# A decoder layer in fp32 on one core: the up-projection's attention half by Strassen from its second output pair on, and the merged rows' Strassen sums formed there and spilled

## The chip, the cores and the metric

The kernel runs on one core of a Trainium2 chip. The metric is the device time of one execution in microseconds; for the kernel before the median of three runs is 2653.76 us (2652.42 to 2656.70). One execution was also taken by the hardware profiler, which gives the page and the trace that are read below. Engines are TensorE (PE in the profile), VectorE (DVE), ScalarE (ACT), GpSimd (POOL) and SyncE (SP), which issues most DMAs.

## What is computed

One layer of a decoder trunk with 512 tokens and a model width of 2048, all in float32:

```
h   = RMSNorm(x)
[u | v_sgu | q | k | v_att | g_a | g_b] = h @ W_in
y_a = u * (tril(W_s) v_norm + b)            # 1024 wide, chunks of 128
y_b = stick-breaking attention(q, k, v_att) # 1024 wide, 8 heads
merged = sigmoid(g_a) * (y_a @ W_up_a) + sigmoid(g_b) * (y_b @ W_up_b)
x  += merged @ W_o
x  += (silu(gate) * up) @ W_ffn_out,   [gate | up] = RMSNorm(x) @ W_ffn_in
x  += sigmoid(RMSNorm(x) @ W_pg) * (p @ W_ple)
```

The change lies in the product `y_b @ W_up_b` (1024 to 2048 channels) and in how `merged` is handed to `W_o`.

## The kernel before

**Numbers and products.** Every float32 operand is kept as two parts that TensorE multiplies at full rate, a high part (ACT copies it into the type fp32r) and a low part (DVE subtracts the high part from the original). A product of two such operands is three matmuls, high by high, high by low and low by high (`mm3`, L296 to L298). Activations stand transposed, channels by tokens. The work is cut into units of 256 input channels by 256 output channels by all 512 tokens. One output pair, 256 output channels, is a `Pair`; a stage has eight of them (j = 0 to 7), or 22 in the FFN.

**Two kinds of unit.** A plain unit ("P") is four blocks of `mm3`, 12 matmuls of 512 columns. A Strassen unit ("S", Winograd's form) cuts the weight unit and the activation into 2 x 2 blocks and makes seven block products instead of eight; with `doubled=7` each is one matmul of 512 columns, which holds high and low part of the right operand side by side, and one of 256, the weight's low part by the high part (L701). So it is 14 matmuls, seven of each size. The seven products collect in PSUM over all units of the pair, and at its end `mix_doubled` (L746 to L797) joins them into the output: four copies on ACT (L757), and on DVE thirteen additions (L760), one of 512 columns and twelve of 256. Weights come two units at a time (a "double"), into one of three slots of high and low parts (`whi_75` and `wlo_76`, `whi_77` and `wlo_78`, `whi_79` and `wlo_80`), four landings ahead of them.

**Weights** (class `Weights`, L320 to L390). A plain double is one load on SP (L339), the high split on ACT (L366) and the low split on DVE (L363), 1024 columns each. A Strassen double is two loads on SP (L341 and L349), an accumulating DMA on POOL (L370) that makes two of the sums, two sums on DVE (L382), and splits of 1280 and of 512 columns.

**Right operands ("forms")** lie in the arena `parts`. A plain form (`plain_form`) takes two blocks of 1024 columns, a Strassen form (`late_form`) a double place of 2 x PLACE = 3584. `plain_first` (L542 on) serves it: the plain blocks are split first, so that plain pairs can use the form; then a second copy of the raw block is loaded, its sums are made on DVE (`tt`, L534), and three of the four sums are split by ACT (L286) and DVE (L287); the fourth sum overwrites a plain block, so it is split only after the form's last plain use (`use_plain`). A pair knows by `until` from which j on its unit is plain or Strassen. `tick()`, called once or more per unit, builds the next waiting form, fetches second copies (`seconds`) and runs actions that `after(n, ...)` put off by n ticks. The tile scheduler then orders each engine's instructions, with manual dependencies that keep the weights and the units in their places.

**The up-projection** (L1376 to L1402). For j = 0 to 7 it makes a pair from the attention half (b) and then one from the gating half (a), four plain units each. For each, the gate's raw block comes from DRAM on SP (`gsp`, L525), is scaled on DVE (`scaled`, L1250) and passed through a sigmoid on ACT (L1383). DVE multiplies it by the two halves of the product straight from PSUM (L1388, twice 512 columns). After a's pair DVE adds both (L1392, 1024 columns), and the merged row is stored to DRAM (L1370, `spill["mix", j]`). After j = 1 to 5 there is a pair of the small product `p @ W_ple` ("ple pair", 12 matmuls, stored on SP).

**W_o's stage** follows. Its right operands `ms` are Strassen forms of the merged rows, loaded from that DRAM copy. `HALF` says how many of its pairs use each plain: the first four rows for one pair, the others for two; the second copies are loaded and summed in the meantime. Its pairs end at L806 (`rest`) and L811 (`onto`). The FFN stage has eight Strassen units per output pair, and one L1430 for each.

## Time and profile before

| | |
|---|---|
| median of three runs | 2653.76 us |
| the profiled execution | 2652.22 us |
| its span in the trace | 2650.5 us |
| TensorE busy | 2635.0 us (99%) |
| VectorE busy | 2255.1 us (85%) |
| ScalarE busy | 1409.0 us (53%) |
| GpSimd busy | 451.5 us (17%) |
| L1392 (end of a j), first and last start | 833.8 and 999.7 us |

The profile counts an instruction as busy from its start to its end; matmuls overlap, so a busy TensorE can still lose time between them. "Idle before" with an arrow names what released an engine that had waited. A row of the timeline gives start, duration, engine, line, operation, output and inputs, sizes and count. L numbers are lines of the kernel before; in the changed kernel the same code stands some lines lower (L363 is L366 there, L366 is L369, L382 L385, L287 L290, L534 L540, L701 L717, L760 L776, L806 L822, L1250 L1266, L1388 L1424, L1392 L1429).

### The profile page before, as it was taken

Reading aid. Unit: us, or ns where it says so; the run is one execution under the profiler, and the core shown is the slowest. Engines: PE = TensorE matmul, PEld = TensorE weight load, DVE = VectorE, ACT = ScalarE, POOL = GpSimd, SP = SyncE. Lnnn points to the kernel's source line nnn. Section 1 sums busy time; section 2 is a strip of 40 time slices with the busy share of each in tenths; the row PEclk is TensorE's granted clock in tenths of the full one; section 3 lists DMA queues with packets and bytes.
Section 4 is the critical chain, followed back from the end, with each engine's and each line's share of the span. In section 5 each row is a group of like instructions: output and inputs, shape, how many; then the busy total and the mean of one; then the engine's idle time right before and its main releaser. Section 6 shows DMA issues by size and latency. Waiting matters only on the chain.

```text
span 2650.5 us, 42355 instructions
## 1 busy us (share of the span) xinstructions
PE 2635.0 (99%) x15202; PEld 2301.7 (87%) x15202; DVE 2255.1 (85%) x3856; ACT 1409.0 (53%) x2245; POOL 451.5 (17%) x559
## 2 busy tenths in 40 slices
PE   9999999999999999999999999999999999999999
PEld 7888888889998888888888888888888888889888
DVE  8687878787887558999888888888889989989898
ACT  7756565655554335466444444444445445455543
POOL 0222223232220001101111111111110211211010
PEclk9999999999999999999999999999999999999999
DMA  6777777677775669988888788888887989988794
GB/s 209 183 195 171 194 172 192 171 192 191 175 195 186 223 224 271 254 246 212 223 213 217 197 203 203 195 212 201 202 203 225 255 227 275 225 242 254 239 269 137
DMA packets 288130, 561.46 MB, mean 212 GB/s; under 512 B 26288, under 2 KB 133552, under 8 KB 287920
## 3 DMA queue, kind: packets, MB, share of 16 engines
q1 hardware_dynamic: 225856, 440.77, 50.6%
q0 software_dynamic: 61776, 117.47, 27.8%
q8 instruction: 119, 1.95, 0.3%
q14 instruction: 91, 0.75, 0.1%
q10 hardware_dynamic: 288, 0.52, 0.1%
HBM read 507.28 MB, written 51.38 MB: 211 GB/s over the span
## 4 chain that ended last, share of the span: by engine, by line
PE 94%; DVE 3%; ACT 1%; DMA 1%; issue 1%; SPq 0%; DVEq 0%; ACTq 0%
PE ps L701 56%; PE ps L298 9%; PE ps L297 9%; PE ps L296 9%; PE small L701 6%; DVE wlo L363 1%; PE small L1181 1%; PE small L1129 1%; PE small L1055 1%; DVE parts L287 1%; DVE wholes L534 0%; DVE wholes L382 0%; PE small L1240 0%; DMA wholes<-x 0%; DMA wholes<-w_ffn_out 0%
## 5 line engine op out<-in xcount | busy, mean ns | idle before, releaser
L701 PE MATMUL ps<-parts,whi 128*128 128x512 f32 x4390 | 1470.6, 398 | 1.9 <-DVE out L806 0.8
L366 ACT ACTIVATE whi<-wholes 128x512 fp32r<-128x512 f32 (+2 forms) x934 | 873.1, 948 | 759.4 <-DVE wholes L382 308.6
L363 DVE TENSOR_TENSOR wlo<-wholes,whi 128x512 fp32r<-128x512 f32 (+2 forms) x934 | 980.8, 1086 | 78.5 <-ACT whi L366 77.6
L701 PEld LDWEIGHTS ps<-parts,wlo 128*128 128x128 f32 x4390 | 823.9, 188 | 188.0 <-DVE wlo L363 2.5
L701 PE MATMUL ps<-parts,wlo 128*128 128x256 f32 x4390 | 868.4, 279 | 1.1 <-DVE wlo L363 1.1
L701 PEld LDWEIGHTS ps<-parts,whi 128*128 128x128 f32 x4390 | 707.2, 189 | 11.3 <-issue 3.1
L297 PE MATMUL ps<-parts,whi 128*128 128x256 f32 (+1 forms) x1622 | 538.4, 332 | 1.0 <-DVE parts L287 0.9
L298 PE MATMUL ps<-parts,wlo 128*128 128x256 f32 (+1 forms) x1622 | 538.3, 333 | 1.1 <-DVE wlo L363 1.1
L296 PE MATMUL ps<-parts,whi 128*128 128x256 f32 (+1 forms) x1612 | 532.5, 332 | 1.8 <-ACT parts L286 1.4
L382 DVE TENSOR_TENSOR wholes<-wholes 128x256 f32<-128x256 f32 x820 | 346.3, 422 | 15.8 <-DVE wlo L363 0.4
L760 DVE TENSOR_TENSOR out<-out,ps 128x256 f32<-128x256 f32 x525 | 216.8, 416 | 152.2 <-ACT out L757 152.0
L297 PEld LDWEIGHTS ps<-parts,whi 128*128 128x128 f32 x1622 | 305.9, 189 | 37.9 <-DVE parts L287 2.9
L298 PEld LDWEIGHTS ps<-parts,wlo 128*128 128x128 f32 x1622 | 306.2, 189 | 30.6 <-DVE wlo L363 1.5
L296 PEld LDWEIGHTS ps<-parts,whi 128*128 128x128 f32 x1612 | 303.5, 189 | 32.2 <-ACT parts L286 2.2
L370 POOL DMA_DIRECT2D wholes<-w_ffn_in x169 | 147.6, 873 | 704.2 <-DVE wholes L382 209.7
L370 POOL DMA_DIRECT2D wholes<-w_in x132 | 117.0, 888 | 543.1 <-DMA wholes<-w_in 112.3
L701 PE MATMUL small<-parts,whi 128*128 128x512 f32 x480 | 190.2, 397 | 0.0
L757 ACT ACTIVATE out<-ps 128x256 f32<-128x256 f32 x279 | 104.7, 385 | 57.0 <-PE ps L701 52.9
L287 DVE TENSOR_TENSOR parts<-wholes,parts 128x1024 fp32r<-128x1024 f32 (+3 forms) x139 | 124.0, 904 | 12.6 <-ACT parts L286 12.5
L286 ACT ACTIVATE parts<-wholes 128x1024 fp32r<-128x1024 f32 (+3 forms) x139 | 107.8, 797 | 46.5 <-DVE wholes L534 32.4
L370 POOL DMA_DIRECT2D wholes<-w_ffn_out x64 | 55.9, 873 | 356.0 <-DMA wholes<-w_ffn_out 84.7
L1428 ACT ACTIVATE out<-out 128x512 f32<-128x512 f32 x44 | 27.9, 633 | 156.2 <-DVE out L1427 156.2
(135 smaller groups left out, 1833.6 us busy)
## 6 DMA issues: line engine op xcount, KB each, us to landing
wholes<-w_ffn_in SPq DMA_DIRECT2D x169, 384.0 KB, 5.6
wholes<-w_in SPq DMA_DIRECT2D x132, 384.0 KB, 5.0
wholes<-w_ffn_in SPq DMA_DIRECT2D x169, 256.0 KB, 4.8
wholes<-w_ffn_in POOLq DMA_DIRECT2D x169, 256.0 KB, 5.4
wholes<-w_in SPq DMA_DIRECT2D x132, 256.0 KB, 4.1
wholes<-w_in POOLq DMA_DIRECT2D x132, 256.0 KB, 5.0
wholes<-w_ffn_out SPq DMA_DIRECT2D x64, 384.0 KB, 6.0
wholes<-x SPq DMA_DIRECT2D x46, 512.0 KB, 6.1
```

The costliest lines, as they stand in the source:

```text
L286: return (nc.scalar.activation(hi, src, AF.Copy), nc.vector.tensor_tensor(out=lo, in0=src, in1=hi.bitcast(F32), op=ALU.subtract))
L287: nc.vector.tensor_tensor(out=lo, in0=src, in1=hi.bitcast(F32), op=ALU.subtract))
L296: nc.tensor.matmul(ps, sh, mh, start=start, stop=False)
L297: nc.tensor.matmul(ps, sh, ml, start=False, stop=False)
L298: return nc.tensor.matmul(ps, sl, mh, start=False, stop=stop)
L363: in_turn(nc.vector.tensor_tensor(out=self.lo[:, blocks], in0=r, in1=h.bitcast(F32), op=ALU.subtract))
L366: in_turn(nc.scalar.activation(h, r, AF.Copy))
L370: nc.gpsimd.dma_start(out=raw[:, 3:5], in_=self.src[:, 1:3], accum_op=ALU.add)
L382: in_turn(nc.vector.tensor_tensor(out=o, in0=x, in1=y, op=ALU.add))
L701: m = nc.tensor.matmul(out, l, r, start=first and k == 0, stop=last and k == 1)
L757: in_turn(nc.scalar.activation(out, x, AF.Copy, scale=scale))
L760: in_turn(nc.vector.tensor_tensor(out=out, in0=x, in1=y, op=op))
```

## The change

- **Attention half by Strassen.** `W_up_b` is planned as "SSSS" for j = 1 to 7, and the four forms of `y_b` become Strassen forms with `until` 1: b's pair is plain at j = 0 and Strassen for the seven pairs after. The pair's result comes out of `mix_doubled` in SBUF, and one multiply of 1024 columns (L1421) takes the place of the two of 512. The second copy of each `y_b` block comes from its DRAM copy.
- **Room.** The four double places for b and the plain blocks for a share the arena `parts`; the high part of a's first form is taken at the arena's other end, behind the last place (`how=("high", "low")`).
- **Sums of the merged rows.** After each j, `leave` makes the row's four Strassen sums on DVE (three instructions, L540: one of 512 columns, two of 256) in the block that held b's part, stores them to DRAM on SP (`sum_spill`, L1436) and then stores the row itself (L1402). W_o's Strassen forms load those sums (L1385 and L1386, 768 and 256 columns) in place of a raw second copy, and only split them. `tick` waits with that load until the sums have been stored, and asks for the smaller rooms.

```diff
--- before.py
+++ after.py
@@ -222,8 +222,11 @@
             builds.popleft().step()
         if seconds:
             f = (urgent or seconds)[0]
-            if (f.used or not any(b.stage == f.stage and b.ready() and not b.there
-                                  for b in builds)) and fits([(wholes, 5 * 256, "old")]):
+            need = [768, 256] if f.sums else [5 * 256]
+            if f.ready_second() and (
+                    f.used or not any(b.stage == f.stage and b.ready() and not b.there
+                                      for b in builds)) and fits(
+                        [(wholes, n, "old") for n in need]):
                 f.fetch_second()
         while waiting and waiting[0][0] <= clock[0]:
             heapq.heappop(waiting)[2]()
@@ -452,12 +455,14 @@
     class Form(Staged):
 
 
-        def __init__(self, kind, steps, sizes, ready, src=None, far=False):
+        def __init__(self, kind, steps, sizes, ready, src=None, far=False, sums=None,
+                     ready_second=lambda: True):
             super().__init__(steps(self))
             self.kind, self.sizes, self.ready = kind, sizes, ready
             self.blocks, self.at_plain, self.used = None, kind == "P", False
             self.src, self.there, self.block, self.due = src, not far, None, 0
             self.second, self.due_second, self.forced, self.stage = None, 0, False, -1
+            self.sums, self.ready_second = sums, ready_second
 
         def fetch(self):
             self.block, self.there, self.due = self.src(), True, clock[0] + WAIT
@@ -469,7 +474,8 @@
         def fetch_second(self):
             if self in seconds:
                 seconds.remove(self)
-            self.second, self.due_second = self.src(5 * 256), clock[0] + WAIT
+            self.second = self.sums() if self.sums else self.src(5 * 256)
+            self.due_second = clock[0] + WAIT
 
         def second_arrived(self):
             if self.forced and self.second is None:
@@ -556,6 +562,15 @@
         yield
         while not form.second_arrived():
             yield
+        if form.sums:
+            t, v = form.second
+            split_into(x[:, 4:7, 0], x[:, 4:7, 1], cut(t.f()))
+            give(t)
+            while not form.used:
+                yield
+            split_into(x[:, 3, 0], x[:, 3, 1], v.f())
+            give(v)
+            return
         w = form.second
         b = cut(w.f())
         if gain:
@@ -603,7 +618,7 @@
         split_into(x[:, 3, 0], x[:, 3, 1], v.f())
         give(v)
 
-    def late_form(src, ready=always, gain=None, far=False):
+    def late_form(src, ready=always, gain=None, far=False, **how):
 
 
 
@@ -615,11 +630,11 @@
             return form.operand()
 
         return Form("S", steps, [(parts, 2 * PLACE, "place"), (wholes, 1024, "low")], ready,
-                    src, far)
-
-    def plain_form(src, ready=always, gain=None, raw=1024, how="low", far=False):
+                    src, far, **how)
+
+    def plain_form(src, ready=always, gain=None, raw=1024, how=("low", "low"), far=False):
         def steps(form):
-            hi, lo = form.blocks = parts.take(1024, how), parts.take(1024, how)
+            hi, lo = form.blocks = tuple(parts.take(1024, h) for h in how)
             w = form.raw()
             if gain:
                 gained(hi.own(), w.f(), *gain)
@@ -636,7 +651,8 @@
             return tuple([x.own(0, T), x.own(T)] for x in form.blocks)
             yield
 
-        return Form("P", steps, [(parts, 1024, how)] * 2 + [(wholes, raw, "low")] * bool(raw),
+        return Form("P", steps,
+                    [(parts, 1024, h) for h in how] + [(wholes, raw, "low")] * bool(raw),
                     ready, src, far)
 
     class Pair:
@@ -1300,7 +1316,8 @@
     def plan_rest():
         for j in range(KU):
             for b in "ba":
-                plan((w_up_a if b == "a" else w_up_b)[j], "PPPP")
+                plan((w_up_a if b == "a" else w_up_b)[j],
+                     "SSSS" if b == "b" and j else "PPPP")
             if 0 < j < 6:
                 planned.append((w_ple[j + 2].rearrange("p (b c) -> p b c", b=4), 1, "P"))
         for j in range(KU):
@@ -1316,9 +1333,11 @@
             plan(w_gate[j], now(GATE, GATE_UNTIL, j))
 
     def y_form(c, i):
-        return plain_form((lambda: y_a[i]) if c == "a" else lambda: load(y_spill[i]),
-                          lambda: len(y_done) == 8, raw=0 if c == "a" else 1024,
-                          far=c == "b")
+        if c == "b":
+            return late_form(lambda n=1024: load(y_spill[i], n), lambda: len(y_done) == 8,
+                             far=True)
+        return plain_form(lambda: y_a[i], lambda: len(y_done) == 8, raw=0,
+                          how=("low" if i else "high", "low"))
 
     ys = {(c, i): y_form(c, i) for c in "ba" for i in range(4)}
     build(ys.values())
@@ -1359,7 +1378,20 @@
     part = {}
     spill = {(n, j): tc.dram_tile([P, 1024], F32, name=nm(n)) for n in ("mix", "x1", "x2")
              for j in range(KU)}
-    there = set()
+    there, sum_spill = set(), {}
+
+    def second_blocks(d):
+        blocks = take(768, "old"), take(256, "old")
+        nc.sync.dma_start(out=blocks[0].f(), in_=d[:, 256:1024])
+        nc.sync.dma_start(out=blocks[1].f(), in_=d[:, 0:256])
+        return blocks
+
+    def summed_form(kind, n, j):
+        if kind == "P":
+            return spilled_form(kind, n, j)
+        d = sum_spill[n, j] = tc.dram_tile([P, 1024], F32, name=nm(n))
+        return spilled_form(kind, n, j, sums=lambda: second_blocks(d),
+                            ready_second=lambda: (n, j, "sums") in there)
 
     def spilled_form(kind, n, j, gain=None, **how):
         return (late_form if kind == "S" else plain_form)(
@@ -1371,7 +1403,7 @@
         there.add((n, j))
         give(block)
 
-    ms = [spilled_form("S", "mix", j) for j in range(KU)]
+    ms = [summed_form("S", "mix", j) for j in range(KU)]
     build(ms)
     for j in range(KU):
         for b in "ba":
@@ -1383,15 +1415,30 @@
                 nc.scalar.activation(g, g, AF.Sigmoid)
 
             after(1, gate)
-            pr = pair([ys[b, i] for i in range(4)], last=j == KU - 1)
-            for h, ps in zip((g[:, :T], g[:, T:]), pr.ends()):
-                nc.vector.tensor_tensor(out=h, in0=h, in1=ps, op=ALU.mult)
+            pr = pair([ys[b, i] for i in range(4)], last=j == KU - 1, j=j,
+                      until=(b == "b",) * 4, doubled=7 * (b == "b"))
+            if pr.n["S"]:
+                nc.vector.tensor_tensor(out=g, in0=g, in1=pr.o, op=ALU.mult)
+            else:
+                for h, ps in zip((g[:, :T], g[:, T:]), pr.ends()):
+                    nc.vector.tensor_tensor(out=h, in0=h, in1=ps, op=ALU.mult)
             if b == "b":
                 part[j] = s
             else:
-                nc.vector.tensor_tensor(out=g, in0=g, in1=part[j].f(), op=ALU.add)
-                give(part.pop(j))
-                after(1, lambda j=j, s=s: store("mix", j, s))
+                other = part.pop(j)
+                nc.vector.tensor_tensor(out=g, in0=g, in1=other.f(), op=ALU.add)
+
+                def leave(j=j, s=s, other=other):
+                    o, x = cut(other.f()), cut(s.f())
+                    tt(o[:, 0:4:3], twice(x[:, 3]), x[:, 1:3])
+                    tt(o[:, 1], o[:, 3], x[:, 1])
+                    tt(o[:, 2], o[:, 1], x[:, 0], ALU.add)
+                    nc.sync.dma_start(out=sum_spill["mix", j], in_=other.f())
+                    give(other)
+                    store("mix", j, s)
+                    there.add(("mix", j, "sums"))
+
+                after(1, leave)
         if not j:
             ple_operands()
         elif j < 6:
```

## The prediction, on record before the changed kernel ran

> **What bounds the kernel now.** I read the page first: the span, the engines, the chain that ended last.
>
> ```profile
> span 2650.5 us, 42355 instructions
> PE 2635.0 (99%) x15202; PEld 2301.7 (87%) x15202; DVE 2255.1 (85%) x3856; ACT 1409.0 (53%) x2245; POOL 451.5 (17%) x559
> PE 94%; DVE 3%; ACT 1%; DMA 1%; issue 1%; SPq 0%; DVEq 0%; ACTq 0%
> ```
>
> The matmul stream is the time: a change pays by taking matmul time off PE, and loses only where PE is made to wait. The profiled run took 2652.22 us, 1.72 around its span and 1.54 below the median 2653.76; the sum below is a difference, put on the median at the end.
>
> Then the stage. First the starts of L1392, which closes each j; then stretches of two j of the up-projection and one FFN output pair (start:end, length, busy time and count of PE, PEld, DVE, ACT, POOL; clock, DMA share, GB/s); then L1430, once per FFN pair of eight Strassen units.
>
> ```profile
> 953.49 1.22 DVE L1392 TENSOR_TENSOR wholes<-wholes 128x1024 f32<-128x1024 f32 x1
> 977.97 1.23 DVE L1392 TENSOR_TENSOR wholes<-wholes 128x1024 f32<-128x1024 f32 x1
> 999.73 1.22 DVE L1392 TENSOR_TENSOR wholes<-wholes 128x1024 f32<-128x1024 f32 x1
> ```
>
> ```profile
> 857.30:881.80 24.50, 24.50 (x109) 20.29 (x109) 16.37 (x20) 9.57 (x12) 0.00 (x0) 1.00 0.65 225
> 1500.00:1519.50 19.50, 19.50 (x113) 17.04 (x112) 17.28 (x32) 9.37 (x13) 3.49 (x4) 1.00 0.76 194
> ```
>
> ```profile
> L1430 DVE TENSOR_TENSOR out<-out x3: 682/684/686, 1505.3 to 1544.4; 128x512 f32<-128x512 f32 x3
> ```
>
> A j takes 24.48 us with a ple pair (96 + 12 matmuls of 512 columns) and 21.76 without: both give 0.2267 us per matmul, at clock 1.00, PE never idle. What PE waits for, in the up-projection (809 to 999.5) and around w_o's start (1000 to 1060):
>
> ```profile
> PE ps L297 <- DVE parts L287: 0.5, 1, 0.5
> PE ps L701 <- DVE out L806: 0.8, 1, 0.8
> ```
>
> **What a Strassen pair saves.** A plain pair of four units is 48 x 0.2267 = 10.88 us. FFN pairs come every (1544.4 - 1505.3) / 2 = 19.55 us for eight units, 9.77 for four. So 1.11 us per pair, 7.8 us for the seven b pairs of j = 1 to 7.
>
> A rule speaks against this. The Trainium skill, page "TensorE: Matmul & The Clock Gate", section "Back-to-back issue gap", gives a sustained spacing of about 131 ns at 512 columns and 81 at 128, so that small matmuls pay a floor; by my estimate from these, about 98 ns at 256, seven products of one of each would cost 1.60 us against 1.57 for twelve of 512, and nothing would be saved. Here it does not hold: 0.2267 us per 512-column matmul, and 14 matmuls in 2.44 us, 0.349 per pair of sizes, hence about 0.12 for the 256-column one. That is nearer the same page's isolated gap, N/2.4 + 2.5, which gives 216 and 109 ns.
>
> **What it costs on DVE.** DVE runs an instruction while the one before drains, so I count steps from start to start:
>
> ```profile
> 812.94 0.42 DVE L760 TENSOR_TENSOR out<-out,ps 128x256 f32<-128x256 f32 x1
> 813.27 0.69 DVE L760 TENSOR_TENSOR out<-ps,out 128x512 f32<-128x512 f32 x1
> 813.87 1.22 DVE L363 TENSOR_TENSOR wlo<-wholes,whi 128x1024 fp32r<-128x1024 f32 x1
> 815.00 1.22 DVE L1250 TENSOR_TENSOR wholes<-wholes 128x1024 f32<-128x1024 f32 x1
> L363 DVE TENSOR_TENSOR wlo<-wholes,whi 128x1280 fp32r<-128x1280 f32 x410 | 609.7, 1487 | 21.4 <-ACT whi L366 20.9
> ```
>
> 0.335 for 256 columns, 0.60 for 512, 1.14 for 1024; so about 1.42 for 1280 and 0.87 for 768 (estimates, by the same 0.07 to 0.08 under a duration). The dear place is the build of b's Strassen operands: their sums and second splits can be made only between the last plain use (j = 0) and the first Strassen use (j = 1). DVE in order, from the last product of b at j = 0 to a's second multiply; before, then now (L540 sums, L290 low halves, L385 and L366 weights, L1424 is old L1388, L1429 old L1392):
>
> ```order
> L363 TENSOR_TENSOR wlo_78<-wholes,whi_77 128x1024
> L287 TENSOR_TENSOR parts<-wholes,parts 128x512 x2
> L1388 TENSOR_TENSOR wholes<-wholes,ps_8366 128x512
> L1388 TENSOR_TENSOR wholes<-wholes,ps_8367 128x512
> L1392 TENSOR_TENSOR wholes<-wholes 128x1024
> ```
>
> ```order
> L366 TENSOR_TENSOR wlo_78<-wholes,whi_77 128x512
> L540 TENSOR_TENSOR wholes<-wholes 128x2x256
> L540 TENSOR_TENSOR wholes<-wholes 128x256 x2
> L1424 TENSOR_TENSOR wholes<-wholes,ps_8381 128x512
> L540 TENSOR_TENSOR wholes<-wholes 128x2x256
> L290 TENSOR_TENSOR parts<-wholes,parts 128x4x256
> L366 TENSOR_TENSOR wlo_76<-wholes,whi_75 128x1024
> L1424 TENSOR_TENSOR wholes<-wholes,ps_8382 128x512
> L540 TENSOR_TENSOR wholes<-wholes 128x256
> L1429 TENSOR_TENSOR wholes<-wholes 128x1024
> L540 TENSOR_TENSOR wholes<-wholes 128x256
> L290 TENSOR_TENSOR parts<-wholes,parts 128x4x256
> ```
>
> The first two forms straddle the end of j = 0; the splits of the third and fourth stand 8 and 10 rows further down, with the spill sums and a gate between. What DVE does there before:
>
> ```profile
> 821.05 2.36 DVE L287 TENSOR_TENSOR parts<-wholes,parts 128x1024 fp32r<-128x1024 f32 x2 [0.26 <-ACT parts L286]
> 831.79 0.69 DVE L1388 TENSOR_TENSOR wholes<-wholes,ps 128x512 f32<-128x512 f32 x1 [0.80 <-PE ps L298]
> 833.08 0.69 DVE L1388 TENSOR_TENSOR wholes<-wholes,ps 128x512 f32<-128x512 f32 x1 [0.60 <-PE ps L298]
> 833.81 1.22 DVE L1392 TENSOR_TENSOR wholes<-wholes 128x1024 f32<-128x1024 f32 x1
> 856.95 1.22 DVE L1392 TENSOR_TENSOR wholes<-wholes 128x1024 f32<-128x1024 f32 x1
> ```
>
> From 813.87 to L1392 of j = 1 at 856.95 it has 43.1 us. Before, 18 steps of 1024, 11 of 512 and 4 of 256 stand there: 28.5 us. Now 4 of 1280, 19 of 1024, 1 of 768, 19 of 512, 30 of 256: 49.7 us. So this queue runs at least 6.6 us late at the end of j = 1. PE does not see all of it. The multiply at 833.08 had waited for the last matmul of j = 0, so b's second pair began near 832.9, and j = 1 ended near 832.9 + 21.76 = 854.6. With no idle on DVE, the first split (19.7 us of steps) is done at 833.6, just after that start; the fourth (31.6 us) at 845.5. With 1 to 3.5 us of waits on ACT and PE, of the kind of the bracketed 0.26, 0.80 and 0.60, the fourth is done at 846.5 to 849. PE fills some of the gap: its order puts the products on unsummed operands first, and eight matmuls of a's pair into b's second double. After the fourth split are still to run some 2.8 us of b's products (four of seven of a 4.88 us double) and 40 matmuls of a, 9.07 us: j = 1 ends at 858.4 to 860.9 if all of them wait for that split, at 853.5 if nothing waits. More of a is drawn forward around the earlier waits, since PE's order holds pieces of both pairs there, so I take 857.5, +2.9, which holds the first saved pair. Bounds: +6.3, and -1.6 with all hidden, the 0.5 at L297, whose splits change in the same stretch, gone too.
>
> In the steady j the mix comes in:
>
> ```order
> L1392 TENSOR_TENSOR wholes<-wholes 128x1024
> L363 TENSOR_TENSOR wlo_80<-wholes,whi_79 128x1024
> L363 TENSOR_TENSOR wlo_78<-wholes,whi_77 128x1024
> L1250 TENSOR_TENSOR wholes<-wholes 128x1024
> L1388 TENSOR_TENSOR wholes<-wholes,ps_8751 128x512
> ```
>
> ```order
> L1429 TENSOR_TENSOR wholes<-wholes 128x1024
> L540 TENSOR_TENSOR wholes<-wholes 128x2x256
> L776 TENSOR_TENSOR out_8924<-out_8924,ps_8882 128x256
> L540 TENSOR_TENSOR wholes<-wholes 128x256
> L776 TENSOR_TENSOR out_8924<-out_8924,ps_8887 128x256
> L540 TENSOR_TENSOR wholes<-wholes 128x256
> L776 TENSOR_TENSOR out_8924<-out_8924 128x256
> ```
>
> The spill sums stand between the first steps of the next mix (old L760), so their store leaves SP some 3 us into b's pair, and the Strassen weights and gates queued behind it on SP wait as long. A j has 7 steps of 1024 and 5 of 512 before, 11.0 us; now 2 of 1280, 6 of 1024, 7 of 512, 18 of 256, 19.9, against a period of 24.48 - 1.11 = 23.37. It fits, with 3.5 us over, so the late queue catches up within two j. The last two hold 22.7 of 23.37 and 19.6 of 20.65. What else DVE waited for in one j before:
>
> ```profile
> 863.92 1.23 DVE L363 TENSOR_TENSOR wlo<-wholes,whi 128x1024 fp32r<-128x1024 f32 x1 [2.60 <-ACT whi L366]
> 867.11 1.23 DVE L1250 TENSOR_TENSOR wholes<-wholes 128x1024 f32<-128x1024 f32 x1 [1.97 <-DMA wholes<-gsp]
> 869.46 1.28 DVE L1388 TENSOR_TENSOR wholes<-wholes,ps 128x512 f32<-128x512 f32 x2 [1.12 <-ACT wholes L1383]
> 875.79 1.23 DVE L363 TENSOR_TENSOR wlo<-wholes,whi 128x1024 fp32r<-128x1024 f32 x1 [2.07 <-ACT whi L366]
> ```
>
> 7.8 us of idle, mostly DVE being early; I price what stays of it at 0.1 us of PE wait per j, 0.7 in all, between 0 and 0.5 each (3.5).
>
> **w_o's start.** The sums of the merged rows leave DVE there, and the 0.8 us at L701 with them: -0.8, between 0 and -1.0. DMA: the up-projection's own traffic (809 to 1000), the page's GB/s by slices, and what a double of Strassen weights takes in the FFN, against a plain one:
>
> ```profile
> DMA packets 12055, 40.51 MB, mean 212 GB/s; under 512 B 1316, under 2 KB 1759, under 8 KB 12044
> ...
> GB/s 209 183 195 171 194 172 192 171 192 191 175 195 186 223 224 271 254 246 212 223 213 217 197 203 203 195 212 201 202 203 225 255 227 275 225 242 254 239 269 137
> ...
> wholes<-w_ffn_in SPq DMA_DIRECT2D x169, 384.0 KB, 5.6
> wholes<-w_ffn_in SPq DMA_DIRECT2D x169, 256.0 KB, 4.8
> wholes<-w_ffn_in POOLq DMA_DIRECT2D x169, 256.0 KB, 5.4
> ...
> wholes<-w_up_b SPq DMA_DIRECT2D x13, 512.0 KB, 5.1
> ```
>
> Fourteen doubles gain 384 KB each, and eight stores of 512 KB come in: 9.7 MB more make 263 GB/s, below the busiest slice's 275. Free, or part of the 0.7. ACT (9.57 of 24.50 us busy) takes the longer high halves and four copies per mix, POOL (0.00) the accumulates: free.
>
> **Sum:** 2.9 - 6 x 1.11 + 0.7 - 0.8 = -3.9; on the profiled run 2648.3, on the median 2649.9. The bounds together: -9.3 to +3.1.
>
> **Rivals.** *The build hides.* PE's reordering covers the queue: -1.6 - 6.7 - 0.8 = -9.1, 2644.7. For it: a's 10.88 us of plain work are there to be drawn forward; against: the 6.6 us overflow, and that the order draws only eight of 48. *DVE becomes the bound* of the stage: the idle of 7.8 us per j stays, since the gates come behind a store that waits for DVE itself. Each us of idle beyond 3.5 costs one per j. From 4.3 us on the change is a loss, from 5.2 on one that a measurement tells (6 x 1.7 + 2.9 - 6.7 - 0.8 = +5.6); at 6 us it is +10.4, 2664.2. For it: the order of store and gates on SP; against: with the queue behind, splits and gates have arrived before DVE gets to them. *The matmul floor*, with nothing saved per pair: +4.0 + 0.7 - 0.8 = +3.9, 2657.7; the rows above leave it 0.03.
>
> **Numbers.** Forecast 0.62, hidden build 0.20, DVE bound 0.15, floor 0.03. A measurement of this kernel tells 0.2%, 5.3 us: under 2648.5 is faster, over 2659.1 slower. Of the forecast's cases about a quarter lie under 2648.5. Faster 0.20 + 0.15 = 0.35; slower 0.12, most of the DVE bound; same 0.53. The range runs from near the hidden build to the early end of the DVE bound: 2645.0 to 2656.5.
>
> **What would show it.** Right: L1429 16 to 23.5 us apart but 24 to 30 at j = 1; PE waits of 3 to 6 us on L290 or L776 in b's second pair and none beyond 0.5 later; no L822 wait at w_o's start. Wrong: waits on L366, L1266 or gates in j = 3 to 7, no wait at j = 1, or pairs not 1.1 us shorter.

## The result, and the profile after

The changed kernel is slower: 2678.4 us against 2656.06 (medians of six runs each), a ratio of 1.0085 with a 95% interval of 1.0075 to 1.0096. The forecast was 2649.9, with a range of 2645.0 to 2656.5. The profiled execution took 2678.21 us, 26.0 more than that of before (2652.22), which lies below all six of its timed runs; so its profile shows a little more loss than the medians do.

From the page of the changed kernel, the span, the engines, and the chain that ended last by engine:

```profile
span 2676.3 us, 42772 instructions
PE 2638.9 (99%) x15258; PEld 2301.1 (86%) x15258; DVE 2317.8 (87%) x3992; ACT 1430.8 (53%) x2292; POOL 465.6 (17%) x573
PE 80%; DVE 9%; DMA 7%; issue 2%; ACT 2%; SPq 0%; DVEq 0%; ACTq 0%; POOLq 0%
```

PE still reads 99% busy. What moved is the chain, from 94% PE to 80%, with 9% DVE and 7% DMA. The add that closes each j (L1429) as a group, with first and last start:

```profile
L1429 DVE TENSOR_TENSOR wholes<-wholes x8: 1218/1222/1227, 839.4 to 1021.0; 128x1024 f32<-128x1024 f32 x8
```

And the one of j = 1, from the timeline:

```profile
871.34 1.23 DVE L1429 TENSOR_TENSOR wholes<-wholes 128x1024 f32<-128x1024 f32 x1
```

Against 833.8, 856.95 and 999.7 before, the add of j = 0 comes 5.6 us later, that of j = 1 14.4 and that of j = 7 21.3. These are DVE's times, and DVE is behind PE here. PE's own last matmul of a's pair (found by its place in the program's order) ends at 861.9 in j = 1 and at 1016.6 in j = 7, against 854.8 and 999.0 before: 7.1 and 17.6 us later. So from j = 1 to 7 PE lost another 10.5 us, where six Strassen pairs should have won 6.7, 17.2 in all. What PE waits for in the up-projection (800 to 1022; in all, times, longest):

```profile
PE ps L717 <- DVE wholes L1424: 5.0, 3, 4.0
PE ps L717 <- DVE wlo L366: 3.3, 3, 1.5
PE ps L299 <- DVE out L776: 2.9, 1, 2.9
PE ps L717 <- ACT out L918: 2.5, 5, 0.8
PE ps L299 <- ACT parts L289: 1.6, 1, 1.6
PE ps L300 <- DVE parts L290: 0.8, 2, 0.5
PE ps L717 <- DVE parts L290: 0.4, 1, 0.4
```

These add up to 16.5 us, where there were 0.5 before. The splits of b's own operands, on which the prediction had set its 2.9, are the 0.4 of the last row. The large ones are a's multiply (L1424), which frees PSUM banks, and the low halves of weights (L366). Both stand in DVE's queue, and what DVE itself waited for longest in this stretch is the gate; first the changed kernel's row, then the one of before (800 to 1000):

```profile
DVE wholes L1266 <- DMA wholes<-gsp: 18.8, 7, 4.0
```

```profile
DVE wholes L1250 <- DMA wholes<-gsp: 13.2, 9, 2.3
```

Why the gate is late shows in the chain that ended last, between j = 5's add and b's and a's multiplies of j = 6 (968 to 1002; start, duration, what):

```profile
972.40 1.14 DVE wholes L1429
...
974.68 0.60 DVE wholes L540
...
976.78 0.42 DVE wholes L540
...
977.24 8.30 DMA mix<-wholes
...
985.55 3.74 DMA wholes<-gsp
...
992.34 1.13 DVE wholes L1421
...
996.62 0.61 DVE wholes L1424
...
997.27 2.52 PE ps L717 x8
```

The add, the spill sums, their store (8.30 us to landing), then the load of the next gate into the block that was just stored, the scaling, the multiplies, and PE. `take(..., "low")` gives the lowest free block, and that is the one whose store is under way: two blocks serve nearly all of the sixteen gates in turn. Before, the block of b's part was free right after the add, with no store behind it. The stores have also become slower, with the sums and the Strassen weights beside them (in the up-projection; KB each, median us to landing; the changed kernel, then the one of before):

```profile
mix<-wholes SPq DMA_DIRECT2D x14, 512.0 KB, 6.3
```

```profile
mix<-wholes SPq DMA_DIRECT2D x7, 512.0 KB, 2.8
```

Three of PE's waits cost more than themselves. In the stretches behind them (start:end, length, busy PE, PEld, DVE, ACT, POOL; granted clock, DMA share, GB/s) the clock is down:

```profile
846.20:851.20 5.00, 4.99 (x17) 4.07 (x18) 3.27 (x4) 1.51 (x2) 0.83 (x1) 0.66 0.71 94
892.00:895.00 3.00, 3.00 (x11) 2.26 (x9) 2.96 (x5) 2.36 (x3) 0.00 (x0) 0.50 0.09 32
997.20:1001.20 4.00, 3.93 (x14) 3.40 (x15) 3.93 (x6) 1.32 (x2) 0.00 (x0) 0.57 0.69 217
```

That is 5.00 x 0.34 + 3.00 x 0.50 + 4.00 x 0.43 = 4.9 us of matmul time, none of which was in the sum. PE, again, shows as busy in them. With the 7.8 us that were saved, PE lost 25.4 us in the up-projection: the waits name 16.0 of them and the clock 4.9, and 4.5 are not named by any view.

Nor does the loss end there. W_o's first and seventh outputs (L811, L827 in the changed kernel) come 16.3 and 18.1 us later than before, and the whole span is 25.8 us longer. So some 8 us of the loss arise behind the up-projection. PE's waits from 1016.6 on add up to 8.8 us there, against 3.3 us from 999.0 on before.

### The profile page after: what moved, and what is told of

Read it like the earlier page. It is cut to its first block, busy times and chain, and to the rows that moved or that the text cites. A ratio compares the mean times of both kernels' runs of the same rounds, so it can differ in the third digit from the quotient of the medians.

```text
span 2676.3 us, 42772 instructions
## 1 busy us (share of the span) xinstructions
PE 2638.9 (99%) x15258; PEld 2301.1 (86%) x15258; DVE 2317.8 (87%) x3992; ACT 1430.8 (53%) x2292; POOL 465.6 (17%) x573
## 4 chain that ended last, share of the span: by engine, by line
PE 80%; DVE 9%; DMA 7%; issue 2%; ACT 2%; SPq 0%; DVEq 0%; ACTq 0%; POOLq 0%
PE ps L717 55%; PE small L717 6%; PE ps L301 5%; PE ps L300 5%; PE ps L299 5%; DVE wlo L366 3%; DVE parts L290 1%; DMA wholes<-gsp 1%; DVE wholes L540 1%; DMA wholes<-x 1%; DMA wholes<-w_o 1%; DMA mix<-wholes 1%; DMA wholes<-hid 1%; DVE out L776 1%; DVE wholes L385 1%
## 5 line engine op out<-in xcount | busy, mean ns | idle before, releaser
L717 PE MATMUL ps<-parts,whi 128*128 128x512 f32 x4558 | 1531.1, 399 | 10.1 <-DVE wholes L1424 5.0
L366 DVE TENSOR_TENSOR wlo<-wholes,whi 128x512 fp32r<-128x512 f32 (+2 forms) x948 | 994.2, 1085 | 40.2 <-ACT whi L369 39.5
L717 PE MATMUL ps<-parts,wlo 128*128 128x256 f32 x4558 | 903.5, 279 | 6.0 <-DVE wlo L366 6.0
L300 PE MATMUL ps<-parts,whi 128*128 128x256 f32 (+1 forms) x1510 | 495.7, 329 | 3.1 <-DVE parts L290 2.9
L301 PE MATMUL ps<-parts,wlo 128*128 128x256 f32 (+1 forms) x1510 | 494.9, 329 | 1.8 <-DVE wlo L366 1.8
L299 PE MATMUL ps<-parts,whi 128*128 128x256 f32 (+1 forms) x1500 | 489.8, 329 | 6.9 <-ACT parts L289 3.0
L385 DVE TENSOR_TENSOR wholes<-wholes 128x256 f32<-128x256 f32 x848 | 359.9, 424 | 23.3 <-DMA wholes<-w_up_b 3.7
L776 DVE TENSOR_TENSOR out<-out,ps 128x256 f32<-128x256 f32 x567 | 234.6, 417 | 157.9 <-ACT out L773 157.5
L717 PE MATMUL small<-parts,whi 128*128 128x512 f32 x508 | 202.1, 398 | 0.0
```

The costliest lines, as they stand in the source:

```text
L299: nc.tensor.matmul(ps, sh, mh, start=start, stop=False)
L300: nc.tensor.matmul(ps, sh, ml, start=False, stop=False)
L301: return nc.tensor.matmul(ps, sl, mh, start=False, stop=stop)
L366: in_turn(nc.vector.tensor_tensor(out=self.lo[:, blocks], in0=r, in1=h.bitcast(F32), op=ALU.subtract))
L385: in_turn(nc.vector.tensor_tensor(out=o, in0=x, in1=y, op=ALU.add))
L717: m = nc.tensor.matmul(out, l, r, start=first and k == 0, stop=last and k == 1)
```

## The experiments

Each kernel was timed beside the kernel before on the same chip (medians of 2654.1 to 2654.7 there), and a ratio is to that. The theory after the traces: **A, the loop** (store, landing, gate load, multiply) makes the waits. Its rival: **B, DVE is simply full** with 20 us of steps per j.

**Sums left out, sums alone.** The first keeps the Strassen half and gives `other` back after L1429:

```diff
-    ms = [summed_form("S", "mix", j) for j in range(KU)]
+    ms = [spilled_form("S", "mix", j) for j in range(KU)]
...
                 nc.vector.tensor_tensor(out=g, in0=g, in1=other.f(), op=ALU.add)
+                give(other)
...
-                    tt(o[:, 0:4:3], twice(x[:, 3]), x[:, 1:3])
-                    tt(o[:, 1], o[:, 3], x[:, 1])
-                    tt(o[:, 2], o[:, 1], x[:, 0], ALU.add)
-                    nc.sync.dma_start(out=sum_spill["mix", j], in_=other.f())
-                    give(other)
                     store("mix", j, s)
-                    there.add(("mix", j, "sums"))
```

> The attention half by Strassen as changed, but no sums of the merged rows in the up-projection: W_o's forms load a raw second copy, as before the change, and the block of b's part is given back right after L1429. Theory A (the loop): a j's next gate is loaded into the block from which the sums are stored, so store, landing, gate load, sigmoid and multiply stand one behind the other, and PE waits for the multiply to free its PSUM banks; the waits from j = 2 on (about 17 us with the slow clock behind them) then nearly go: 2660 to 2667 us, about 14 less than the change's 2678. Theory B (DVE full): DVE's own 20 us of steps per j make the waits; this kernel takes only 1.3 us per j off, so 2670 to 2677.

Measured: 2670.5, ratio 1.0057 (1.0042 to 1.0072). Eight us less, at the low end of B. DVE's and PE's longest waits:

```profile
DVE wholes L1266 <- DMA wholes<-gsp: 21.3, 8, 4.8
PE ps L717 <- DVE parts L290: 7.0, 2, 6.4
```

The gate is as late as ever, but all of DVE's waits for it, save one of 1.0 us at the start, are now for b's gate, which has no store before it: it goes into the block that L1429 has just read, so it is loaded behind the add, and it takes 5.3 to 9.8 us to land. a's gate still stands behind the row's store, but DVE waits for it nowhere. So the loop closes without a store too: add, load, landing, multiply. Its price on PE fell all the same. From j = 1 to 7 PE takes 143.8 us instead of 154.7, so 6.3 are lost there instead of 17.2. The build of b's operands took much of that back, with a single wait of 6.4 us for a split; j = 1 ends on PE at 868.1 instead of 861.9. A's number failed, and this run alone does not tell A from B.

The second keeps the sums and their stores and leaves b plain:

```diff
-                     "SSSS" if b == "b" and j else "PPPP")
+                     "PPPP")
...
-            return late_form(lambda n=1024: load(y_spill[i], n), lambda: len(y_done) == 8,
-                             far=True)
+            return plain_form(lambda: load(y_spill[i]), lambda: len(y_done) == 8, far=True)
...
-                          how=("low" if i else "high", "low"))
+                          how=("low", "low"))
...
-            pr = pair([ys[b, i] for i in range(4)], last=j == KU - 1, j=j,
-                      until=(b == "b",) * 4, doubled=7 * (b == "b"))
+            pr = pair([ys[b, i] for i in range(4)], last=j == KU - 1, j=j)
```

> The other half alone: b stays plain in all eight pairs, and the merged rows' sums are made and stored in the up-projection. Theory A: the next gates come late here too, but DVE makes the sums at once, since no mix stands between them, and plain pairs leave four PSUM banks over, so PE hardly waits: 2654 to 2661, against 2656 before. Theory B: DVE has 12 us of steps per j: 2652 to 2657, the 0.8 us at the start of W_o gained. If the sums cost by their DMA traffic alone: 2662 or more.

Measured: 2655.57, ratio 1.0000 (0.9991 to 1.0010), as both theories had it.

Its adds as a group, and DVE's wait for gates:

```profile
L1428 DVE TENSOR_TENSOR wholes<-wholes x8: 1224/1224/1225, 833.8 to 999.7; 128x1024 f32<-128x1024 f32 x8
```

```profile
DVE wholes L1266 <- DMA wholes<-gsp: 8.8, 6, 2.6
```

The loop is there, and the adds of the first and last j come where they did before, to 0.1 us. With 12 us of steps per j DVE makes the sums at once. DVE waits 8.8 us for gates in all, and PE for none of them.

**The loop opened, DVE as full as ever.**

```diff
-            s = load(gate_spill[b, j], 1024, "low")
+            s = load(gate_spill[b, j], 1024, "old")
```

> The change, with the gates' blocks taken from the room that was given back longest ago instead of from the lowest free one, so that some gate loads no longer wait for the store of the sums (the room is nearly full of rows fetched for W_o, so not all of them). Theory A: a part of the loop opens, 2666 to 2675. Theory B: 2676 to 2681, nothing changes.

Measured: 2656.53, ratio 1.0009 (0.9999 to 1.0019): 22 us back, more than A had allowed, and nothing of B. Of the 22.3 us between the two profiled spans, 14.5 lie in the up-projection; the others lie behind it, and no run shows by what way they came. What DVE waits for the gate, and what PE waits for:

```profile
DVE wholes L1266 <- DMA wholes<-gsp: 3.5, 3, 2.3
PE ps L299 <- DVE out L776: 3.2, 2, 2.9
PE ps L299 <- ACT parts L289: 1.6, 1, 1.6
PE ps L300 <- DVE parts L290: 0.8, 2, 0.5
PE ps L717 <- DVE parts L290: 0.7, 1, 0.7
```

A steady stretch of about one j, in the columns of the table of stretches:

```profile
935.00:959.00 24.00, 24.00 (x120) 20.33 (x119) 21.13 (x35) 11.30 (x17) 1.74 (x2) 1.00 0.78 249
```

DVE is busy 21.1 of 24 us there, and PE 24 of 24. L1429 stands at 935.25 and 958.62 around it:

```profile
935.25 1.22 DVE L1429 TENSOR_TENSOR wholes<-wholes 128x1024 f32<-128x1024 f32 x1
958.62 1.23 DVE L1429 TENSOR_TENSOR wholes<-wholes 128x1024 f32<-128x1024 f32 x1
```

They are 23.37 us apart, the 24.48 - 1.11 of the prediction to the second digit. So the Strassen pair is worth what was forecast and DVE can bear it. What is left of the waits is at j = 0 and 1, but for 0.3 us.

The control, the same line in the kernel before the change:

> A control: the kernel before the change with its gates taken from the oldest room. DVE has 11 us of steps per j there and PE waits for no gate, so the loop should not be felt: 2652 to 2657, no difference. If the oldest room is better by itself (other places for everything that is loaded): 2645 to 2651, and then what moving the gates gave back is not the loop alone.

Measured: 2657.03, ratio 1.0009 (1.0000 to 1.0019). The oldest room wins nothing by itself. With this run four kernels make a square: loop or not, DVE at 11 or at 20 us per j. Only both together cost: 2657.0 and 2655.6 with DVE at 11 to 12, 2656.5 and 2678.4 with DVE at 20.

**One gate only.** First the sums in a block of their own, so that b's block is free after the add:

```diff
+                give(other)
...
-                def leave(j=j, s=s, other=other):
+                def leave(j=j, s=s):
+                    other = take(1024, "old")
```

> The change, gates from the lowest free room as there, but the sums are made in a block of their own (the one given back longest ago) and the block of b's part is given back right after L1429, so that the next b gate can be loaded at once; the a gate still waits for the store of the row, as before the change. Theory A (the loop through the block): 2655 to 2661, as with the gates moved. Rival C: the gates moved to the oldest room helped by something else (other places for all rows, another order on SP), and this kernel stays at 2670 to 2679.

Measured: 2672.71, ratio 1.0065 (1.0050 to 1.0081). A's number failed. The gate's wait on DVE stayed at 21.7 us, and the build waits as in the kernel without sums:

```profile
DVE wholes L1266 <- DMA wholes<-gsp: 21.7, 8, 3.9
PE ps L717 <- DVE parts L290: 8.2, 2, 7.6
```

The chain that ended last shows which gate it is (from j = 5's add on):

```profile
971.75 1.15 DVE wholes L1429
...
972.92 0.33 SPq L1402
...
973.29 9.62 DMA wholes<-gsp
...
982.94 1.23 DVE wholes L1266
```

It is b's gate, loaded right behind the add with no store to wait for, and 9.62 us on its way. a's gate is loaded behind the row's store (6.5 and 8.3 us after it at j = 4 and 5), but DVE waits for it nowhere, as without the sums. With DVE's steps as in the changed kernel, PE's loss from j = 1 to 7 fell from 17.2 to 7.6 us; so some 10 us of it came from the store before b's gate, and that is not DVE's fullness.

Then only a's gates moved:

```diff
-            s = load(gate_spill[b, j], 1024, "low")
+            s = load(gate_spill[b, j], 1024, "old" if b == "a" else "low")
```

> The change, with only a's gates taken from the oldest room; b's keep the lowest free one, into which they are loaded behind the store of the sums or of the row. Giving b's block back early did not help by itself (2672.7). If a's gate, which is loaded behind the other store and asked for last, holds the loop: 2655 to 2662. If either gate behind a store is enough to hold it: 2666 to 2677.

Measured: 2671.36, ratio 1.0065 (1.0051 to 1.0079), a wait of 16.5 us for gates. So b's gate behind a store is enough to hold the loop, and a's gate is not what holds it. The profiled executions, by the end of PE's last matmul of a's pair (us; without any loss j = 1 to 7 would take 144.2 - 6.7 = 137.5):

| kernel | j = 1 | j = 7 | between | rest of the span |
|---|---|---|---|---|
| before | 854.8 | 999.0 | 144.2 | 1651.5 |
| changed | 861.9 | 1016.6 | 154.7 | 1659.7 |
| without the sums | 868.1 | 1011.9 | 143.8 | 1655.9 |
| sums in a block of their own | 869.8 | 1014.9 | 145.1 | 1658.8 |
| a's gates moved | 863.4 | 1017.4 | 154.0 | 1651.4 |
| both gates moved | 863.7 | 1002.1 | 138.4 | 1651.9 |

Only with both moved does next to nothing of the loop remain (0.9 us). The times of whole kernels hide this, because the part behind the up-projection differs by up to 8 us as well.

**What is left, the build at j = 0 and 1.** More time for it, b plain at j = 1 too; first with the gates as changed, then with moved gates:

```diff
-                     "SSSS" if b == "b" and j else "PPPP")
+                     "SSSS" if b == "b" and j > 1 else "PPPP")
...
-                      until=(b == "b",) * 4, doubled=7 * (b == "b"))
+                      until=(2 * (b == "b"),) * 4, doubled=7 * (b == "b"))
```

> The change with b plain at j = 0 and 1 and Strassen from j = 2, so that the sums and second splits of its four operands have 22 us more to be made in. If the build of the operands costs some 9 us of waits at j = 0 and 1, as the trace suggests: 2669 to 2673 (7 less, 1.1 more for one Strassen pair fewer). If those waits are mostly the same loop as later, or come back one j later: 2676 to 2681.

Measured: 2664.15, ratio 1.0034 (1.0019 to 1.0048): 14 us off instead of 5 to 9, with 20.4 us of gate waits still there. But of the 14.2 us between the two profiled spans only 3.8 lie in the up-projection (PE ends j = 7 at 1012.8); the others lie behind it, and no run says why. So this run does not show what the build costs.

> Gates from the oldest room, and b Strassen from j = 2 only. What is left of PE's waits with the gates moved is 7.7 us at j = 0 and 1, where the operands are built. If the build is short of time there, 22 us more take off some 5 of them, for 1.1 of a Strassen pair fewer: 2650 to 2654, below the kernel before (2655). If the build only moves its waits to j = 2: 2656 to 2659.

Measured: 2656.91, ratio 1.0010 (1.0001 to 1.0019), the second case: no gain on moved gates alone. PE's longest wait stands near j = 2 now, for a bank that ACT empties of the ple pair (L918):

```profile
PE ps L717 <- ACT out L918: 2.3, 2, 1.8
```

Moved gates without the four operands' sums, which leaves out part of the computation (the raw blocks are split in place of their sums):

```diff
+        if form.bare:
+            if not form.used:
+                split_into(x[:, 4:7, 0], x[:, 4:7, 1], b[:, 1:4])
+                while not form.used:
+                    yield
+                split_into(x[:, 3, 0], x[:, 3, 1], b[:, 0])
...
         tt(b[:, 4], b[:, 3], b[:, 2])
```

> Gates from the oldest room, and the four b operands are built without their sums: the raw blocks are split where the sums would be, so 4 x 1.27 = 5.1 us of DVE steps are gone from j = 0 and 1 and with them part of the computation. Second loads, splits and rooms stay. If the 8 us of waits left at j = 0 and 1 are DVE's queue: 2651 to 2654. If they are the second loads, the rooms or PSUM: 2655 to 2658.

Measured: 2653.85, ratio 0.9999 (0.9990 to 1.0008), 2.7 below the kernel with the sums, though the two ratios' intervals overlap. PE ends j = 1 6.1 us earlier (857.6 instead of 863.7) and j = 7 1.1 us earlier. So DVE's steps make the wait at j = 1, but most of what they give there is lost again by j = 7, beginning with a wait of 2.3 us for the ple pair's bank.

Moved gates without the spill sums:

> Gates from the oldest room, b Strassen from j = 1, and no sums of the merged rows in the up-projection. If the sums, once they hold up no gate, are worth what they take off the start of W_o: 2657 to 2660, 1 to 3 above the kernel with sums. If they cost as much DVE in the up-projection as they save: 2655 to 2657, the same.

Measured: 2662.41, ratio 1.0030 (1.0020 to 1.0041): the sums, once they hold up no gate, are worth some 6 us, more than forecast. The adds of this kernel, then those of the one with sums:

```profile
L1429 DVE TENSOR_TENSOR wholes<-wholes x8: 1215/1222/1226, 840.6 to 1005.5; 128x1024 f32<-128x1024 f32 x8
```

```profile
L1429 DVE TENSOR_TENSOR wholes<-wholes x8: 1215/1219/1226, 841.3 to 1005.6; 128x1024 f32<-128x1024 f32 x8
```

The up-projection ends at nearly the same time in both, on PE too (1003.0 and 1002.1), so what the sums win they win behind it.

Two operands from j = 1, two from j = 2:

```diff
-                     "SSSS" if b == "b" and j else "PPPP")
+                     now("SSSS", (1, 1, 2, 2), j) if b == "b" else "PPPP")
...
-                      until=(b == "b",) * 4, doubled=7 * (b == "b"))
+                      until=(1, 1, 2, 2) if b == "b" else None, doubled=7 * (b == "b"))
...
-                nc.vector.tensor_tensor(out=g, in0=g, in1=pr.o, op=ALU.mult)
+                nc.vector.tensor_tensor(out=g, in0=g, in1=pr.out(), op=ALU.mult)
```

> Gates from the oldest room, and the first two operands Strassen from j = 1, the other two from j = 2; the pair of j = 1 mixes plain and Strassen units. If the waits at j = 1 come from the third and fourth operand, whose splits are last: 2650 to 2654, about 0.5 below the kernel with all four from j = 2. If the first two make them, or the mixed pair's own ending costs more: 2655 to 2659.

Measured: 2651.77, ratio 0.9987 (0.9979 to 0.9996). This one beats both kernels, by 0.13% of the one before. It is the best of sixteen tries, and its interval ends close to 1.

```profile
PE ps L717 <- ACT out L918: 1.8, 1, 1.8
PE ps L299 <- ACT parts L289: 1.5, 1, 1.5
PE ps L300 <- DVE parts L290: 1.1, 3, 0.5
PE ps L717 <- DVE wholes L1424: 1.1, 2, 0.6
```

The 3.2 us on L776 are gone, and what is left is small. Two things changed at once, though: a pair that mixes plain and Strassen units has no doubled products, so at j = 1 it also holds fewer PSUM banks and ends by another mix. Which of the two took the wait away is not shown.

**By which way a late gate reaches PE.** a's pair before b's from j = 1, with moved gates:

```diff
-            for b in "ba":
+            for b in "ab" if j else "ba":
```

> Gates from the oldest room, and from j = 1 on a's plain pair before b's Strassen pair, so that 10.9 us of plain work stand between the last plain and the first Strassen use of b's operands, with all seven Strassen pairs kept. If the build is short of time only: some 5 of the 8 us of waits go, 2649 to 2653, below the kernel before. If DVE is so far behind that the waits move to a's weights or to the next pair: 2655 to 2659.

Measured: 2667.31, ratio 1.0049 (1.0037 to 1.0062), above both cases, although DVE waits for gates much less than in the changed kernel (7.7 us against 18.8). PE's longest wait:

```profile
PE ps L299 <- DVE out L776: 7.8, 4, 3.6
```

A Strassen pair with doubled products holds six large banks of PSUM and a small one, so the plain pair behind it cannot begin until the mix has emptied some. Theory D: the banks are the way. The same kernels with high and low part in separate matmuls (four banks, 21 matmuls of 256 columns a unit):

```diff
-                      until=(b == "b",) * 4, doubled=7 * (b == "b"))
+                      until=(b == "b",) * 4, doubled=0)
```

> The change, but b's Strassen pairs with high and low part of the right operand in separate matmuls (21 of 256 columns a unit, 2.53 us by the trace, against 2.44 with 14): 2.5 us less saved over seven pairs, but four PSUM banks instead of six and one small one, and about 2.3 us fewer DVE steps per mix. Theory D (banks): a Strassen pair that needs all six large banks cannot run past a plain pair whose multiply waits for its gate; with four it can, so PE's waits on L1424 and on L918 (7.5 us and the slow clock after them) go, and 2664 to 2670. If late gates hold PE through DVE's queue alone (weights split behind a waiting L1266): waits on L366 stay, 2670 to 2677.

Measured: 2672.74, ratio 1.0068 (1.0054 to 1.0081). The waits on L1424 are gone as D had it, but the time went to the other way that was foreseen, weights behind the gate in DVE's queue, and to a bank of the ple pair:

```profile
DVE wholes L1266 <- DMA wholes<-gsp: 17.4, 8, 6.8
PE ps L301 <- DVE wlo L366: 4.1, 2, 3.0
PE ps L299 <- ACT out L918: 2.7, 1, 2.7
```

> The same with the gates from the oldest room. Theory D: the 3.2 us of waits on L776 at j = 1 go with their slow clock, for 2.5 us of less saving: 2653 to 2656, 1 to 3 below the kernel with moved gates alone (2656.5). If those waits come from DVE's queue and not from the banks: 2657 to 2660.

Measured: 2660.63, ratio 1.0019 (1.0010 to 1.0028), above both cases. PE waits for no mix any more (it stands on L743 in this form), and 2.0 us on weights came; with less saved per pair it is a loss.

> Gates from the oldest room, a's pair first from j = 1 on, and four banks. With six banks this order cost 11 us more than b first, and 7.8 of its 10.9 us of waits were on L776, which empties b's banks for the plain pair behind. Theory D: they go, 2651 to 2656. If the order itself puts DVE behind: 2662 to 2668, and the waits move to weights or gates.

Measured: 2658.0, ratio 1.0014 (1.0005 to 1.0023), 9 below the same order with six banks, and no wait for the mix; 3.4 us on operands' splits in its place. The wait went as D had it, and the number lies between the two cases. That it is the banks is not shown alone: this form also takes some 2.3 us of DVE steps off each mix.

> The fastest so far (gates from the oldest room, two operands Strassen from j = 1 and two from j = 2; 2651.8) with four banks. Its waits in the up-projection are few (L918 1.8, L1424 1.1): theory D takes those and some slow starts, 3 us, against 2.1 us of less saving: 2649 to 2653. If they are not the banks': 2653 to 2656.

Measured: 2657.46, ratio 1.0008 (0.9999 to 1.0017), above both cases: this form of the pair costs more than the 2.1 us counted.

## Why the prediction was wrong

In the terms of the sum, on the profiled executions: the build's 2.9 became 7.1, the steady j's 0.7 became 17.2, and W_o's -0.8 became 8.2 for all that follows the up-projection. With the 6.7 saved that is 25.8, the difference of the two spans.

- **The saving per pair** (1.11 us, 7.8 in all): right. The steady 23.37 us of the kernel with moved gates show it. The Trainium skill, page "TensorE: Matmul & The Clock Gate", section "Back-to-back issue gap", gives the sustained spacing by which, in the prediction's estimate, small matmuls would have eaten it; the 23.37 us are evidence against that spacing for this stream.
- **The build, +2.9**: too small, and by another route. PE ended j = 1 at 861.9, not at 857.5, 7.1 us later than before and past the upper bound of 6.3. I had PE wait for the splits of the third and fourth operand. It waited 0.4 us there; 2.9 went on a bank that the mix, queued on DVE behind sums and splits, emptied late, some 1.7 on the clock behind that, and 2.4 on the first splits, which cost 0.5 before.
- **The steady j, +0.7 between 0 and 3.5**: the step that failed. I wrote that the 7.8 us of idle in one j before were "mostly DVE being early", and that with the queue behind, "splits and gates have arrived before DVE gets to them". They had not: a gate is loaded into the block of DVE's last add, behind that add and behind the store of what is in it, so a DVE that is behind makes its own inputs late. I counted the store as leaving SP some 3 us into b's pair; the block is free only when it has landed, 6.3 us later (median), and the gate then takes 5.1 us more (median). From j = 1 to 7 PE lost 17.2 us, where I had 0.7 and at most 3.5; moving the gates took all but 0.9 of it away. It was the rival "DVE becomes the bound", for which the text named this very order on SP, at a chance of 0.15 and a price of 10.4 at 6 us of idle; and its name was not right either, since DVE at 21 of 24 us is no bound (shown by the moved gates).
- **W_o's start, -0.8**: not gained in the changed kernel. What follows the up-projection took 8.2 us more than before, and waits name 5.5 of them (8.8 against 3.3 us); why they came is not shown. PE's wait at W_o's start (1016 to 1240) still stands:

```profile
PE ps L717 <- DVE out L822: 0.6, 1, 0.6
```

- **DMA, "free, or part of the 0.7"**: 51 MB moved at 240 GB/s, as reckoned in size. But a store's landing went from 2.8 to 6.3 us (medians), and landings were what the loop is made of. A mean rate below a busiest slice says nothing of a latency.
- **The clock**: the sum took every wait at its length. The three stretches above add 4.9 us. The Trainium skill, page "TensorE: Matmul & The Clock Gate", Part 1, has the clock at half rate after an idle window of about 3.4 us, and back after as much work. The half rate agrees (0.50 at 892). The length does not quite: the stretch at 892 follows two waits on weights of 1.5 and 0.8 us, with work between them:

```profile
889.79 0.50 PE L717 MATMUL ps<-parts,wlo 128*128 128x256 f32 x2 [1.54 <-DVE wlo L366]
891.52 0.50 PE L717 MATMUL ps<-parts,wlo 128*128 128x256 f32 x2 [0.77 <-DVE wlo L366]
```

The waits on the splits of b's operands differ between kernels: 0.4 us as changed, up to 6.4 and 7.6 without the sums and with sums in a block of their own. A good part is the same gate. In the latter two DVE stands 2.9 and 3.9 us at L1266 directly ahead of the splits of the third and fourth operand (849.75 and 850.59), because b's gate is loaded behind j = 0's add; in the changed kernel the gate of j = 1 has a block that was free before, and DVE does not wait for it (842.61).

Open: the rest of that difference (4.3 us at the longest without the sums and with moved gates, where DVE does not wait for this gate either), and the stages behind the up-projection, which take from 2 us less to 8 us more than before in these kernels, only in part by waits that name a cause.

## What to carry to other kernels

Before an engine with slack is filled, ask which of its inputs come from what it did one round earlier, through a load into the same block and perhaps a store before it; the slack that one sees may be what pays for that loop. A free list that hands out the block just given back puts the engine's own last step, and any store of it, in front of the next load. Handing out the one given back longest ago cost one word here and gave 22 us back. When a whole kernel's time does not fit a theory, follow the engine that bounds it from stage to stage: here two changes in different stages hid each other.

And count the PSUM banks of a pair that replaces a smaller one. With six large ones held, PE waited 5.0 us at a's late multiply. With four, in a form that differs in more than that, the wait was gone, but the late gate held PE through the weights behind it in DVE's queue, and little of the time came back (2672.7 against 2678.4).

## What was not expected of the hardware

- The granted clock read 0.66 over 5 us behind a wait of 2.9 us, 0.57 over 4 us behind one of 4.0, and 0.50 over 3 us behind two waits of 1.5 and 0.8 us less than 2 us apart; that cost 4.9 us in a stage of some 200.
- A store of 512 KB landed in 2.8 us (median) before and in 6.3 after, while the mean rate in the up-projection went only from 212 to 240 GB/s. It was 3.2 with the sums alone (230 GB/s) and 6.5 with the Strassen weights and no sums (227 GB/s), so it goes with those weights; packets under 2 KB were 2514 and 4956 there. Which property of the weights' loads does it is not shown.
